# Finer first units, larger unit groups where two layers meet, and copies that go to ScalarE first

## The chip, the cores and the metric

The kernel runs on one core of one Trainium2 chip. The metric is the device time of one execution in microseconds (us); a time given for a kernel is the median of several executions. Besides, one execution was recorded by the hardware profiler, and its times are those of the views below. Engines go by short names: PE is TensorE (PEld its weight loads), DVE is VectorE, ACT is ScalarE, SP is SyncE, whose queue issues the loads.

## The reference

Two layers run one after the other on 256 tokens of 2048 numbers. Each layer normalizes x over its 2048 numbers, scales and shifts it by vectors made from a conditioning vector c (h), projects h to 6144 columns, runs two branches on them, projects the concatenation of both back to 2048 columns, normalizes that and adds it, gated, to x:

```python
    mod = (c @ w_ada + b_ada)[:, None, :]
    shift, scale, gate = jnp.split(mod, 3, axis=-1)
    h = rms_norm(x, g_pre) * (1 + scale) + shift
    z = h @ w_in
    u, g_pool, q, k, v, g_diff = jnp.split(z, splits, axis=-1)
    pool_out = multiscale_pool(u, w_pool, pool_scale) * jax.nn.silu(g_pool)
    ...
    diff_out = att.reshape(B, S, D_DIFF) * jax.nn.silu(g_diff)
    y = jnp.concatenate([pool_out, diff_out], axis=-1) @ w_out
    return x + (1 + gate) * rms_norm(y, g_post)
```

So a layer cannot start before the one ahead of it has ended for a token: its norm needs all 2048 numbers of y, and h needs the norm of the new x. Everything is float32; the result is (256, 2048).

## The kernel before, in words

**Tiles.** The 256 tokens are two row tiles of 128 (`st` 0 and 1). The 2048 rows of a weight matrix are 16 k tiles of 128; two neighbouring k tiles are one `kp`. The columns come in blocks of 512: 12 blocks (`nb`) for w_in, 4 for w_out. A *unit* is one kp of one block, 128 x 1024 numbers, 512 KB. For each unit SP loads a tile `raw`, ScalarE rounds it to a short float (`whi`, CAST), VectorE makes the rest (`wlo` = raw - whi), and TensorE multiplies: per k tile and row tile the three products hi*hi, hi*lo and lo*hi, 12 products of 128x512 per unit. The left operand `h` is split into hi and lo as well: x is scaled by its row's norm (`xnt`), transposed on TensorE into a bank of PSUM (`psb`), and ScalarE applies the k tile's scale A and shift B twice (`hz`, then `hft`), from which VectorE makes the lo part.

**Modulation.** The vectors shift, scale and gate are 48 pieces of 128 per layer, each made by two reductions on VectorE of loaded tiles of w_ada (`adaz`, 512 KB each) with the spread c (`cb`). A k tile of h needs four such tiles, then three small instructions (A, A, B).

**Visits.** The modulation comes in little by little, so kp after kp becomes available. The planner (`plan`) goes round the 12 blocks and takes as many kp as there are. Each such *visit* of a block has one sum of 128x512 per row tile in PSUM (`accc`, four of them): sums are copied out to SBUF at a visit's end (`zz`) and copied in again (`accc<-zz`) when the block's next visit starts. Such copies go to VectorE or ScalarE, whichever the planner holds less loaded (`lighter`, `copy`).

**Order.** The order of instructions on each engine is written out ahead of time, by a planner in the program (`Flow`): parts of the kernel are tasks, each with a due time, and a cost model chooses which task issues next on an engine. Each engine then executes its list in order and waits on semaphores. `need(u, before)` is the due time so many us ahead of TensorE's use of unit u. Buffers come from `Slots`: 34 large SBUF tiles for raw, whi, wlo, w_ada, h and results, with shares by kind.

**The turn.** In the last visit of w_out (four units), all products of row tile 0 come ahead of those of row tile 1 (`group`), and so they do for the first four units of layer 1. At a row tile's last product follow: a square with a sum on ScalarE (`sqj`) and the gating (`yz`) on VectorE, a norm of about ten tiny steps on VectorE (`rs`, `rx`, `ry`, `rh`), four updates of x, squares of x, another norm (`rms`), and `half_h`, which scales, transposes and modulates 256 columns of this row tile. Its due times before were those of the units that use it.

**The start.** SP loads c, x and eight w_ada tiles, then the weights. The squares of x go in eight pieces to whichever engine is lighter, one norm serves both row tiles, and `make_h` makes the first kp for both.

## Time and profile before

| what | value |
|---|---|
| median of 3 runs | 863.91 us (862.27 to 865.26) |
| profiled execution, its own time | 866.97 us |
| its span, first to last instruction | 865.2 us |
| mean granted TensorE clock | 0.977 |
| TensorE busy | 802.3 us, 93% |
| VectorE busy | 742.6 us, 86% |
| ScalarE busy | 509.9 us, 59% |
| loaded from HBM | 242.17 MB |

In the profile every instruction has one line (L125, the place in the planner that issues it), so groups go by the names of tiles: `accc<-whiz,hz` is a product of layer input and rounded weights into a sum, `accc<-whiz,catz` one of w_out, `psb<-consts,xnt` a transpose of scaled x. In rows of the timeline stand the start, the length, the engine, the operation, what is written from what, and in brackets how long the engine had been idle and what ended that. Matmuls are pipelined: the starts tell the pace, the lengths overlap. A row of the table by stretches has the busy time of each engine in it, the granted clock, the share of the DMA engines and what they moved.

### The profile page before, as it was taken

How to read it: one execution, taken by the hardware profiler on the slowest of the kernel's cores; microseconds unless marked ns; L12 is line 12 of the kernel's file. 1: busy time of each engine (PE TensorE's matmuls, PEld its weight loads, DVE VectorE, ACT ScalarE, POOL GpSimd, SP SyncE). 2: the span in 40 equal slices, each digit the busy share in tenths (PEclk: the TensorE clock that was granted, in tenths of full speed). 3: DMA queues.
4: the chain of work that ended last, by engine and by line, in shares of the span. 5: the costliest groups of instructions: out<-in, count | busy, mean ns of one | idle time of the engine just before them, and what ended most of it. 6: DMA issues, size and time to landing. Idle time of an engine off the chain costs nothing.

```text
span 865.2 us, 11872 instructions
## 1 busy us (share of the span) xinstructions
PE 802.3 (93%) x4058; PEld 667.1 (77%) x4058; DVE 742.6 (86%) x1375; ACT 509.9 (59%) x871; POOL 0.2 (0%) x4
## 2 busy tenths in 40 slices
PE   3699999999999999999719999999999999999995
PEld 1588888879788887888607788787888788788884
DVE  6999999999999989999998898998657697787335
ACT  4777787567455687654467544546544684784341
POOL 0000000000000000000000000000000000000000
PEclk9999999999999999999958999999999999999998
DMA  9988899999999667689966999999666444636602
GB/s 344 410 341 300 315 370 390 393 339 404 403 327 402 246 206 276 195 323 393 348 227 225 361 364 381 382 398 358 226 203 212 147 126 149 230 115 193 210 0 98
DMA packets 68239, 245.08 MB, mean 283 GB/s; under 512 B 7729, under 2 KB 8017, under 8 KB 67665
## 3 DMA queue, kind: packets, MB, share of 16 engines
q1 hardware_dynamic: 67890, 244.14, 78.3%
q8 instruction: 32, 0.52, 0.2%
q14 instruction: 29, 0.24, 0.1%
q10 hardware_dynamic: 288, 0.17, 0.1%
HBM read 242.17 MB, written 2.11 MB: 282 GB/s over the span
## 4 chain that ended last, share of the span: by engine, by line
PE 37%; DVE 8%; DMA 4%; issue 2%; ACT 2%; DVEq 0%; SPq 0%; ACTq 0%
PE accc L125 33%; PE psb L125 4%; DVE adaz L125 3%; DVE wloz L125 3%; DMA rawz<-in_w_in 2%; DMA adaz<-in_w_ada 2%; DVE x L125 1%; DVE yz L125 0%; ACT xnt L125 0%; ACT whiz L125 0%; ACT hz L125 0%; DVE rh L125 0%; ACT hft L125 0%; DVE ry L125 0%; ACT zz L125 0%
## 5 line engine op out<-in xcount | busy, mean ns | idle before, releaser
L125 PE MATMUL accc<-whiz,hz 128*128 128x512 f32 x1280 | 408.2, 396 | 2.1 <-ACT hz L125 2.0
L125 ACT CAST whiz<-rawz 128x1024 fp32r<-128x1024 f32 x256 | 264.3, 1051 | 97.8 <-DMA rawz<-in_w_in 49.8
L125 DVE TENSOR_TENSOR wloz<-rawz,whiz 128x1024 fp32r<-128x1024 f32 x256 | 305.9, 1218 | 15.6 <-ACT whiz L125 12.7
L125 PEld LDWEIGHTS accc<-whiz,hz 128*128 128x128 f32 x1280 | 242.0, 190 | 54.4 <-ACT hz L125 2.9
L125 PE MATMUL accc<-wloz,hz 128*128 128x512 f32 x640 | 253.1, 396 | 1.6 <-DVE wloz L125 1.6
L125 DVE SCALAR_TENSOR_TENSOR adaz<-adaz,cb 128x1024 f32<-128x1024 f32 x192 | 229.2, 1218 | 7.2 <-DMA adaz<-in_w_ada 5.3
L125 PE MATMUL accc<-whiz,catz 128*128 128x512 f32 x512 | 161.1, 393 | 0.0
L125 PEld LDWEIGHTS accc<-wloz,hz 128*128 128x128 f32 x640 | 121.6, 190 | 27.7 <-DVE wloz L125 3.5
L125 PEld LDWEIGHTS accc<-whiz,catz 128*128 128x128 f32 x512 | 95.4, 188 | 19.2 <-issue 0.3
L125 PE MATMUL accc<-wloz,catz 128*128 128x512 f32 x256 | 100.5, 393 | 0.0
L125 ACT COPY zz<-accc 128x512 f32<-128x512 f32 x100 | 57.6, 587 | 65.8 <-PE accc L125 63.7
L125 ACT COPY accc<-zz 128x512 f32<-128x512 f32 x82 | 48.3, 595 | 42.7 <-DVE rtt L125 26.9
L125 PE MATMUL accc<-hz,whiz 128*128 128x256 f32 x512 | 72.1, 283 | 0.0
L125 PEld LDWEIGHTS accc<-hz,whiz 128*128 128x128 f32 x512 | 66.9, 191 | 1.1
L125 PEld LDWEIGHTS accc<-wloz,catz 128*128 128x128 f32 x256 | 48.2, 188 | 10.2 <-issue 0.5
L125 PE MATMUL psb<-consts,xnt 128*128 128x128 f32 x64 | 13.4, 326 | 44.7 <-ACT xnt L125 34.6
L125 PEld LDWEIGHTS psb<-consts,xnt 128*128 128x128 f32 x64 | 8.8, 163 | 50.1 <-ACT xnt L125 39.0
L125 DVE COPY accc<-zz 128x512 f32<-128x512 f32 x44 | 30.1, 687 | 17.7 <-ACT zz L125 17.5
L125 PE MATMUL accc<-hz,wloz 128*128 128x256 f32 x256 | 42.0, 284 | 0.0
L125 DVE COPY zz<-accc 128x512 f32<-128x512 f32 x42 | 28.6, 685 | 8.3 <-PE accc L125 8.2
L125 PEld LDWEIGHTS accc<-hz,wloz 128*128 128x128 f32 x256 | 35.5, 192 | 0.0
L125 DVE TENSOR_TENSOR yz<-accc,Gwg 128x512 f32<-128x512 f32 x16 | 10.7, 687 | 27.9 <-ACT sqj L125 27.8
(104 smaller groups left out, 556.2 us busy)
## 6 DMA issues: line engine op xcount, KB each, us to landing
adaz<-in_w_ada SPq DMA_DIRECT2D x192, 512.0 KB, 7.1
rawz<-in_w_in SPq DMA_DIRECT2D x192, 512.0 KB, 6.7
rawz<-in_w_out SPq DMA_DIRECT2D x64, 512.0 KB, 4.4
x<-in_x SPq DMA_DIRECT2D x2, 1024.0 KB, 8.1
Gwg<-in_w_pool SPq DMA_DIRECT2D x8, 256.0 KB, 8.1
Gwg<-gate SPq DMA_DIRECT2D x2, 1024.0 KB, 5.3
out<-x SPq DMA_DIRECT2D x8, 256.0 KB, 2.8
band<-in_band SPq DMA_DIRECT2D x1, 544.0 KB, 6.9
```

Source lines behind the costliest of these rows:

```text
L125: return f(*args, **kw)
```

## The change

The planner gets other rules and numbers; what is computed stays.

- The first three units (`TURN[0]`, all of kp 0) form a group that goes by single k tiles: k tile 0 with row tile 0, then row tile 1, then k tile 1. Their weights are loaded in halves (`first_loads`), and x's second row tile is loaded behind the first four w_ada tiles. Each row tile has its own squares, norm and `half_h`. Casts and wlo of these units go by halves (`pieces`).
- Where the layers meet, the last two visits of w_out (eight units) form a group, and the first nine units of layer 1 (three kp of three blocks; `START[1]`, `TURN[1]`), sorted by kp. The third pair of sums of such a group takes banks of the transposes.
- `end_out`, `residual` and `half_h` at the turn have fixed early due times (-3, -2, -2.5) and so go ahead of everything else that an engine could issue.
- A copy goes to VectorE only if the planner has it more than 0.5 us behind ScalarE's time.
- The order of w_in's blocks (`ORDERS`) is another, w_out starts with the attention's kp (`HALVES`), the slot shares and some constants of the cost model differ.

```diff
@@ -357,10 +360,11 @@
         self.a, self.out = a, out
         pool = lambda name, **kw: ctx.enter_context(tc.tile_pool(name=name, bufs=1, **kw))
         self.cp, self.sp = pool("cp"), pool("sp")
-        self.big = Slots(f, pool("zp"), "z", self.BIG, raw=3, w=6, ada=3)
+        self.big = Slots(f, pool("zp"), "z", self.BIG, raw=3, hi=3, lo=3, ada=2)
         self.tmp = Slots(f, pool("tp"), "t", self.TMP)
         self.wide = Slots(f, pool("gp"), "g", 1)
         self.banks = Slots(f, pool("psp", space=PSUM), "b", self.BANKS)
+
         self.accs = Slots(f, pool("accp", space=PSUM), "c", self.ACCS)
         self.dp = pool("dp", space=bass.MemoryType.DRAM)
         self.names = 0
...
@@ -380,11 +384,13 @@
         return self.banks.take([P, 512], "ps")
 
 
-    START = [1, 2]
+    START = [1, 3]
+
+    TURN = [3, 9]
     RATE = {(0, 2): 0.82, (1, 2): 0.85, (0, 0): 0.92, (0, 1): 0.9, (1, 0): 0.8, (1, 1): 0.35}
-    ORDERS = [[6, 4, 8, 10, 2, 0, 7, 5, 9, 11, 3, 1]] * 2
-
-    HALVES = ((0, 4), (4, 8))
+    ORDERS = [[6, 4, 7, 5, 2, 8, 9, 3, 10, 11, 0, 1]] * 2
+
+    HALVES = ((4, 8), (0, 4))
 
     def plan(self):
 
...
@@ -443,17 +449,18 @@
                 for kp in range(k0, k1):
                     u = Unit("w_out", l, nb, 2 * kp, kp == k0 and (not late or nb < 2), kp == k1 - 1 and (late or nb < 2), nb < 2 and late)
                     u.end = late
-                    if n == 7:
-                        u.group = 2 * l + 1
+                    if n >= 6:
+                        u.group = 2 * l + 2
                     units.append(u)
                     if n < 6:
                         earn(self.RATE[l, 1])
             while l + 1 < DEPTH and kp_at[l + 1][self.START[l + 1] - 1] is None:
                 take()
-        for l in range(1, DEPTH):
+        for l, n in enumerate(self.TURN):
             i = next(i for i, u in enumerate(units) if u.l == l)
-            for u in units[i : i + 4]:
-                u.group = 2 * l
+            units[i : i + n] = sorted(units[i : i + n], key=lambda u: u.k)
+            for u in units[i : i + n]:
+                u.group = 2 * l + 1
         return units
 
     def lay_out(self):
...
@@ -466,20 +473,24 @@
             while g and i + n < len(self.units) and self.units[i + n].group == g:
                 n += 1
             us = self.units[i : i + n]
-            for sts in ([[0], [1]] if g else [[0, 1]]):
-                self.steps += [(u, sts) for u in us]
+            if g == 1:
+
+                self.steps += [(u, [st], [0]) for st in range(NST) for u in us] + [(u, [0, 1], [1]) for u in us]
+            else:
+                for sts in ([[0], [1]] if g else [[0, 1]]):
+                    self.steps += [(u, sts, [0, 1]) for u in us]
             i += n
         for i, u in enumerate(self.units):
             if u.first:
                 open_[u.w, u.nb] = Visit(u, i)
                 self.visits.append(open_[u.w, u.nb])
             u.visit = open_[u.w, u.nb]
-            u.left = NST
+            u.left = 2 * NST
         for n in range(len(self.steps) - 1, -1, -1):
             self.steps[n][0].step = n
         self.cum = [0.0]
-        for u, sts in self.steps:
-            self.cum.append(self.cum[-1] + 1.36 * len(sts))
+        for u, sts, ks in self.steps:
+            self.cum.append(self.cum[-1] + 0.68 * len(sts) * len(ks))
         self.first_use, self.uses = {}, {}
         for u in self.units:
             key = u.w, u.l, u.k // 2
...
@@ -530,20 +540,20 @@
-        for st in range(NST):
-            nc.sync.dma_start(self.x[st], a["x"][st * P : (st + 1) * P, :])
+        self.arrived = [False] * NST
+        f.spawn(self.first_loads, -95.0)
-            f.spawn(lambda st=st: self.first_squares(st), -80.0 + st)
+            f.spawn(lambda st=st: self.first_squares(st), -85.0)
-        f.spawn(self.rope_tables, -60.0)
-        f.spawn(self.mask, -50.0)
+        f.spawn(self.rope_tables, self.need(self.first_end[0]["w_in"], 60.0))
+        f.spawn(self.mask, self.need(self.first_end[0]["w_in"], 60.0))
...
@@ -556,6 +566,31 @@
             f.spawn(lambda l=l: self.load_pool_weights(l))
             for kp in range(8):
                 f.spawn(lambda l=l, kp=kp: self.make_h(l, kp), self.need_h(l, kp, 4.0))
+
+    def first_loads(self):
+
+        us = [u for u in self.units if u.group == 1]
+
+        def x(st):
+            self.nc.sync.dma_start(self.x[st], self.a["x"][st * P : (st + 1) * P, :])
+            self.arrived[st] = True
+
+        def raw(u, i):
+            self.nc.sync.dma_start(tiles[u][:, i], self.a[u.w][u.l, u.nb][:, u.k + i])
+            u.raw = tiles[u]
+
+        tiles = {u: self.big.take([P, 2, NB], "raw", kind="raw") for u in us}
+        x(0)
+        for e in self.adas[:4]:
+            self.ada_tile(e)
+        raw(us[0], 0)
+        x(1)
+        for u in us[1:]:
+            raw(u, 0)
+        for e in self.adas[4:8]:
+            self.ada_tile(e)
+        for u in us:
+            raw(u, 1)
 
     def spread_c(self):
 
...
@@ -669,7 +704,7 @@
     def lighter(self):
 
         now = self.f.now
-        return "vector" if now["vector"] < now["scalar"] else "scalar"
+        return "vector" if now["vector"] + 0.5 < now["scalar"] else "scalar"
 
     def copy(self, out, x):
         if self.lighter() == "vector":
...
@@ -722,6 +757,8 @@
+        if e in self.adas[:8]:
+            return [-81.0, -6.0, -6.0, -6.0, -4.0, -4.0, -4.0, -4.0][self.adas.index(e)]
...
@@ -785,14 +826,22 @@
-        for j in range(4):
-            self.square(0, st, j)
-        self.squared[0][st] = 1
-        if all(self.squared[0]):
-            s1 = self.small([P, NST], "xs1")
-            self.nc.vector.tensor_reduce(s1, self.xss[0], axis=AX.X, op=ALU.add)
-            r = self.rsqrt(s1, NST, 1.0 / D)
-            self.xr[0] = [r[:, st : st + 1] for st in range(NST)]
+        f, x, ss = self.f, self.x[st], self.xss[0]
+        f.wait(lambda: self.arrived[st])
+        n = D if st == 0 else D // 2
+        junk = self.big.take([P, D], "junk", BF16)
+        self.nc.scalar.activation(junk[:, 0:n], x[:, 0:n], AF.Square, accum_out=ss[:, st, 0:1])
+        self.big.give(junk)
+        if st:
+
+            junk = self.big.take([P, n], "junk")
+            self.nc.vector.scalar_tensor_tensor(junk, x[:, n:], 1.0, x[:, n:], op0=ALU.mult, op1=ALU.mult, accum_out=ss[:, st, 1:2])
+            self.big.give(junk)
+            f.due(-4.5)
+            self.xr[0][st] = self.rms(ss[:, st, 0:2])
+        else:
+            f.due(-80.0)
+            self.xr[0][st] = self.rsqrt(ss[:, st, 0:1], 1, 1.0 / D)
...
@@ -806,14 +855,14 @@
-        early = l and kp < self.START[l]
-
-        f.wait(lambda: self.gated[l - 1][0] >= 2 and self.made[l] > 2 * kp + bool(early) if l else not kp or self.made[l] > 2 * kp)
+        early = kp < self.START[l]
+
+        f.wait(lambda: self.gated[l - 1][0] >= 2 and self.made[l] > 2 * kp + bool(early) if l else early or self.made[l] > 2 * kp)
-                f.spawn(lambda st=st: self.half_h(l, kp, st, hi, lo), self.need_h(l, kp, 6.0))
+                f.spawn(lambda st=st: self.half_h(l, kp, st, hi, lo), st + 0.1 * kp - (2.5 if l else 5.5))
...
@@ -848,21 +897,35 @@
         self.tmp.give(xn)
         hf = self.tmp.take([P, 2, P], "hf")
         c = slice(st * P, (st + 1) * P)
+
+        def rest(i):
+            nc.vector.tensor_tensor(lo[:, i, c], hf[:, i, :], hi[:, i, c].bitcast(F32), op=ALU.subtract)
+            self.h_lo.add((l, 2 * kp + i, st))
+
         for i in range(2):
             kt = 2 * kp + i
+            f.wait(lambda: self.made[l] > kt)
             self.modulated(hi[:, i, c], l, kt, b[:, i * P : (i + 1) * P])
             self.h_hi.add((l, kt, st))
             self.modulated(hf[:, i, :], l, kt, b[:, i * P : (i + 1) * P])
+            if not l:
+                rest(i)
         self.banks.give(b)
-        for i in range(2):
-            nc.vector.tensor_tensor(lo[:, i, c], hf[:, i, :], hi[:, i, c].bitcast(F32), op=ALU.subtract)
-            self.h_lo.add((l, 2 * kp + i, st))
+        if l:
+            rest(0), rest(1)
         self.tmp.give(hf)
 
 
+    def pieces(self):
+
+        us = [u for u in self.units if u.group == 1]
+        return [(u, slice(i, i + 1)) for i in range(2) for u in us] + [(u, slice(0, 2)) for u in self.units if u.group != 1]
+
     def load(self):
 
         for u in self.units:
+            if u.group == 1:
+                continue
             self.f.due(self.need(u, 7.0))
             raw = self.big.take([P, 2, NB], "raw", kind="raw", keep=4)
             self.nc.sync.dma_start(raw, self.a[u.w][u.l, u.nb][:, u.k : u.k + 2, :])
...
@@ -870,22 +933,26 @@
 
     def cast(self):
 
-        for u in self.units:
-            self.f.due(self.need(u, 1.5))
+        for u, ks in self.pieces():
+            self.f.due(-5.0 + 1.5 * ks.start if u.group == 1 else self.need(u, 1.5))
             self.f.wait(lambda: u.raw is not None)
-            hi = self.big.take([P, 2, NB], "whi", F32R, kind="w", keep=4)
-            self.nc.scalar.copy(hi, u.raw)
-            u.hi = hi
+            self.f.wait(lambda: self.big.count.get("hi", 0) - self.big.count.get("lo", 0) < 4)
+            if u.hi is None:
+                u.hi = self.big.take([P, 2, NB], "whi", F32R, kind="hi", keep=3)
+            self.nc.scalar.copy(u.hi[:, ks], u.raw[:, ks])
+            u.hi_of |= set(range(2)[ks])
 
     def rest(self):
 
-        for u in self.units:
-            self.f.due(self.need(u, -0.2))
-            self.f.wait(lambda: u.hi is not None)
-            lo = self.big.take([P, 2, NB], "wlo", F32R, kind="w", keep=4)
-            self.nc.vector.tensor_tensor(lo, u.raw, u.hi.bitcast(F32), op=ALU.subtract)
-            self.big.give(u.raw)
-            u.lo = lo
+        for u, ks in self.pieces():
+            self.f.due(-5.0 + 1.5 * ks.start if u.group == 1 else self.need(u, -0.2))
+            self.f.wait(lambda: ks.start in u.hi_of)
+            if u.lo is None:
+                u.lo = self.big.take([P, 2, NB], "wlo", F32R, kind="lo", keep=1)
+            self.nc.vector.tensor_tensor(u.lo[:, ks], u.raw[:, ks], u.hi[:, ks].bitcast(F32), op=ALU.subtract)
+            u.lo_of |= set(range(2)[ks])
+            if ks.stop == 2:
+                self.big.give(u.raw)
 
     def prepare(self):
 
...
@@ -893,7 +960,8 @@
-                acc = self.accs.take([P, NB], "acc")
+                wide = u.group % 2 and not v.more and [w for w in self.visits if w.l == v.l and self.units[w.at].group == u.group].index(v) > 1
+                acc = (self.banks if wide else self.accs).take([P, NB], "acc")
...
@@ -902,13 +970,13 @@
-        for n, (u, sts) in enumerate(self.steps):
+        for n, (u, sts, ks) in enumerate(self.steps):
-            self.mm(u, sts)
-            u.left -= len(sts)
+            self.mm(u, sts, ks)
+            u.left -= len(sts) * len(ks)
...
@@ -917,25 +985,25 @@
-            if u.last and sts:
+            if u.last and ks[-1] and sts:
-                f.spawn(lambda u=u, sts=sts: end(u, sts), self.need(self.units[nxt.at], 3.0))
+                f.spawn(lambda u=u, sts=sts: end(u, sts), -3.0 if u.group and u.w == "w_out" else self.need(self.units[nxt.at], 3.0))
-    def mm(self, u, sts):
+    def mm(self, u, sts, ks):
-        for i in range(2):
+        for i in ks:
-            f.wait(lambda: have(self.h_hi, kt) and u.hi is not None)
+            f.wait(lambda: have(self.h_hi, kt) and i in u.hi_of)
-            if turned or u is self.units[0]:
+            if turned or u.group == 1:
...
@@ -1017,7 +1088,7 @@
-            self.accs.give(acc[st])
+            self.give_sum(acc[st])
```

33 lines of the change are left out of this document (20 added, 13 removed).

## The prediction

> **What bounds the kernel now.** I read the page first: busy shares, then the row of granted clock.
>
> ```profile
> span 865.2 us, 11872 instructions
> PE 802.3 (93%) x4058; PEld 667.1 (77%) x4058; DVE 742.6 (86%) x1375; ACT 509.9 (59%) x871; POOL 0.2 (0%) x4
> ...
> PEclk9999999999999999999958999999999999999998
> ```
>
> TensorE is busy 93% of the span, and its clock is full except in one place just past the middle. So the time is TensorE's work plus the holes in it. The list of waits says whom the holes belong to (total us, times, longest), and one row of it, ScalarE's, is for later:
>
> ```profile
> PE psb L125 <- ACT xnt L125: 34.6, 6, 12.0
> PE psb L125 <- DVE xnt L125: 10.0, 1, 10.0
> ...
> ACT whiz L125 <- DMA rawz<-in_w_in: 49.8, 39, 4.8
> ```
>
> Nearly all are waits of transposes (psb) for a normalized piece of x (xnt). The table by stretches shows where (busy us of PE, weight loads, DVE, ACT, POOL; clock; DMA share; GB/s):
>
> ```profile
> 0.00:20.00 20.00, 7.63 (x9) 2.67 (x9) 13.50 (x60) 8.70 (x17) 0.20 (x4) 1.00 0.90 340
> 20.00:40.00 20.00, 10.93 (x48) 8.81 (x49) 18.30 (x31) 12.86 (x17) 0.00 (x0) 1.00 1.03 409
> ...
> 100.00:120.00 20.00, 20.00 (x103) 17.06 (x102) 19.85 (x34) 16.23 (x26) 0.00 (x0) 1.00 1.02 371
> ...
> 420.00:440.00 20.00, 8.38 (x37) 6.28 (x35) 19.37 (x52) 9.96 (x20) 0.00 (x0) 0.75 0.95 350
> 440.00:460.00 20.00, 6.93 (x21) 5.09 (x22) 17.63 (x46) 13.81 (x34) 0.00 (x0) 0.50 0.46 157
> ```
>
> Holes: the start, and the turn from layer 0 to layer 1. Between them TensorE is full, but so is VectorE (19.85 of 20 us), and the DMA engines are full at the start and at 100 us: gains must not ask more of these two. One product of 128x512 is issued every 0.227 us at full clock, from a piece of the chain that ended last (start, length, count):
>
> ```profile
> 784.02 71.24 PE accc L125 x314
> ```
>
> A unit, 12 such products, is thus 2.72 us, and half of it (one row tile) 1.36 us.
>
> **The start.** The timeline of the first 41 us:
>
> ```profile
> 8.65 0.69 DVE L125 SCALAR_TENSOR_TENSOR junkt<-x 128x512 f32<-128x512 f32 x1 [2.78 <-DMA x<-in_x]
> ...
> 9.95 0.58 ACT L125 COPY cb<-psb 128x512 f32<-128x512 f32 x1 [1.12 <-PE psb L125]
> ...
> 23.24 1.05 ACT L125 CAST whiz<-rawz 128x1024 fp32r<-128x1024 f32 x1 [4.81 <-DMA rawz<-in_w_in]
> ...
> 24.52 1.04 ACT L125 CAST whiz<-rawz 128x1024 fp32r<-128x1024 f32 x1 [0.23 <-DMA rawz<-in_w_in]
> ...
> 25.00 1.22 DVE L125 SCALAR_TENSOR_TENSOR adaz<-adaz,cb 128x1024 f32<-128x1024 f32 x1
> ...
> 26.72 0.34 DVE L125 TENSOR_SCALAR xnt<-x,ry 128x256 f32<-128x256 f32 x1
> ...
> 29.36 0.56 ACT L125 ACTIVATE hz<-psb,B,A 128x256 fp32r<-128x256 f32 x1
> 29.97 2.13 PE L125 MATMUL accc<-whiz,hz 128*128 128x512 f32 x4 [1.95 <-ACT hz L125]
> ...
> 40.41 0.40 PE L125 MATMUL accc<-whiz,hz 128*128 128x512 f32 x1
> ```
>
> The first product comes at 29.97, three units are done at 40.4. One scaling of x (26.72) waits on VectorE behind eight reductions of modulation tiles (adaz), although four suffice for the first k tile. VectorE there, before:
>
> ```order
> L125 SCALAR_TENSOR_TENSOR adaz_136,mod_96<-adaz_136,cb_84 128x1024
> L125 SCALAR_TENSOR_TENSOR adaz_138,mod_96<-adaz_138,cb_84 128x1024
> L125 SCALAR_TENSOR_TENSOR A_98<-mod_96,b_108 128x1
> L125 TENSOR_TENSOR A_98<-A_98,cols_90 128x1
> L125 SCALAR_TENSOR_TENSOR B_100<-mod_96,cols_90 128x1
> L125 TENSOR_SCALAR xnt_232<-x_10_93,ry_220 128x256
> ```
>
> and in the change, around the first three values A, A, B (ry_207 is row tile 0's norm; the last of eight tiny steps stands first here):
>
> ```order
> L126 SCALAR_TENSOR_TENSOR ry_207<-rh_206,ry_207 128x1
> L126 SCALAR_TENSOR_TENSOR adaz_130,mod_94<-adaz_130,cb_84 128x1024
> L126 SCALAR_TENSOR_TENSOR adaz_132,mod_94<-adaz_132,cb_84 128x1024
> L126 SCALAR_TENSOR_TENSOR adaz_134,mod_94<-adaz_134,cb_84 128x1024
> L126 SCALAR_TENSOR_TENSOR A_96<-mod_94,b_107 128x1
> L126 TENSOR_TENSOR A_96<-A_96,cols_90 128x1
> L126 SCALAR_TENSOR_TENSOR B_98<-mod_94,cols_90 128x1
> L126 TENSOR_TENSOR wloz_248<-rawz_103,whiz_138 128x512
> ```
>
> The first product now needs one row tile's norm, four tiles and half a weight tile. Sum: ScalarE's copies of c end at 10.5 (9.95 + 0.58); the square of 2048 columns, estimated from the 1024-column cast, 2.1, to 12.6; eight small steps of about 0.22 to 14.5; three reductions at 1.15 from start to start to 17.9; A, A, B 0.6; then hz 0.4: first product at 19, 11 us earlier. The loads allow it: 512 KB land every 1.28 us (23.24 to 24.52), and behind x (8.65) four such tiles and a quarter megabyte of weights land by about 14.7. But x's second half now queues behind them on SP's ring and lands near 17.4; its square, norm and scaling then share VectorE with the small wlo pieces and give row tile 1 its first product near 25.5. The second k tile needs the next four reductions, which stand behind that norm: 24.1 to 29.0, A and B to 29.6, products from 30.1 on, all 36 of the three units done near 35.0. So 11 us at the first product are worth **5.4 us** at the third unit (40.4 - 35.0). Bounds: 8 if VectorE has less in its way; 1.5 if the extra small instructions and the late second half cost what three reductions do.
>
> **The turn.** The timeline, all engines:
>
> ```profile
> 426.88 0.39 PE L125 MATMUL accc<-whiz,catz 128*128 128x512 f32 x1
> ...
> 432.81 2.74 DVE L125 SCALAR_TENSOR_TENSOR x<-yz,ry,x 128x512 f32<-128x512 f32 x4
> ...
> 438.29 0.91 ACT L125 ACTIVATE xnt<-x,ry 128x256 f32<-128x256 f32 x2 [1.48 <-DVE ry L125]
> 438.86 1.11 PE L125 MATMUL psb<-consts,xnt 128*128 128x128 f32 x4 [11.59 <-ACT xnt L125]
> ...
> 446.89 1.21 DVE L125 SCALAR_TENSOR_TENSOR adaz<-adaz,cb 128x1024 f32<-128x1024 f32 x1
> ...
> 451.41 1.31 ACT L125 ACTIVATE xnt<-x,ry 128x256 f32<-128x256 f32 x3 [5.56 <-DVE ry L125]
> 451.97 1.11 PE L125 MATMUL psb<-consts,xnt 128*128 128x128 f32 x4 [12.00 <-ACT xnt L125]
> 453.21 0.80 PE L125 MATMUL accc<-whiz,hz 128*128 128x512 f32 x1
> ...
> 461.63 0.62 PE L125 MATMUL accc<-whiz,hz 128*128 128x512 f32 x2
> ```
>
> Two waits of 11.59 and 12.00 us, then half clock. From 427.1 to 462.1 are 35.0 us, in which 16 products (3.6 us) and 16 transposes (1.11 for four at half clock, so about 2 at full) get done: **29.4 us lost**. The second wait is one of order. TensorE before, at the end of layer 0 (catz) and the start of layer 1 (hz):
>
> ```order
> L125 MATMUL accc_4044<-whiz_3999,catz_3722 128x512
> L125 MATMUL psb_4285<-consts_86,xnt_4281 128x128 x2
> L125 MATMUL psb_4287<-consts_86,xnt_4282 128x128 x2
> L125 MATMUL psb_4353<-consts_86,xnt_4345 128x128 x2
> L125 MATMUL psb_4355<-consts_86,xnt_4346 128x128 x2
> L125 MATMUL accc_4124<-whiz_4095,hz_4036 128x512
> ```
>
> The other row tile's transposes (4353, 4355) stand ahead of all products of the first. In the change its first ones (psb_4382) come after 26 products of layer 1:
>
> ```order
> L126 MATMUL psb_4252<-consts_86,xnt_4243 128x128 x2
> L126 MATMUL accc_4106<-whiz_4027,hz_4057 128x512
> ```
>
> ```order
> L126 MATMUL accb_4274<-whiz_4235,hz_4058 128x512
> L126 MATMUL psb_4382<-consts_86,xnt_4376 128x128 x2
> L126 MATMUL psb_4384<-consts_86,xnt_4377 128x128 x2
> L126 MATMUL accb_4274<-wloz_4326,hz_4058 128x512
> ```
>
> The chain itself, where nothing else is on VectorE, is read at the end of the kernel:
>
> ```profile
> 854.86 0.39 PE L125 MATMUL accc<-whiz,catz 128*128 128x512 f32 x1
> ...
> 858.57 2.74 DVE L125 SCALAR_TENSOR_TENSOR x<-yz,ry,x 128x512 f32<-128x512 f32 x4
> ```
>
> Last product to first update of x: 3.7 us. Update to scaled x: 432.81 to 438.29, 5.5. Scaled x to product: 451.41 to 453.21, 1.8. Together 11.0. Eight units of one row tile now follow row tile 0's last product, 8 x 1.36 = 10.9 us: its chain is just covered, less what is put into it (two weight casts on ScalarE, one wlo): I take 1.5 us of wait. Row tile 1's chain is 9.8 us up to its transposes (3.7, 5.5 and 438.29 to 438.86); one wlo and six small lo parts stand in it, which I take as two rows like that at 446.89, 2.6: about 12.4. It has 1.5 us of that wait and 26 products, 5.9, plus transposes and lo waits of about 1.5: that leaves **3.5 us**, by this count. The clock comes on top, since short holes cost it too:
>
> ```profile
> 178.78 0.95 PE L125 MATMUL psb<-consts,xnt 128*128 128x128 f32 x4 [1.43 <-ACT xnt L125]
> ...
> 493.68 0.95 PE L125 MATMUL psb<-consts,xnt 128*128 128x128 f32 x4 [1.85 <-ACT xnt L125]
> ...
> 495.00:496.00 1.00, 1.00 (x4) 0.81 (x3) 1.00 (x2) 0.86 (x2) 0.00 (x0) 0.50 1.02 414
> ```
>
> After 1.43 us the clock stayed; after 1.85 it was halved in the second that follows, for some 3.4 us, so 1.6 lost. I add 1.6 once. Turn after: 1.5 + 3.5 + 1.6 = 6.6, **23 us saved**; bounds 16 (another 7 us of wait) and 27 (2.6 left). The Trainium skill ("TensorE: Matmul & The Clock Gate", the clock gate) puts the drop after about 3.4 us of idleness in a free-running window; the row at 493 shows it after 1.85. By the page the 1.6 would not fall due and the time would be 1.6 lower.
>
> **The copies.** Groups, busy us and mean ns:
>
> ```profile
> L125 ACT COPY zz<-accc 128x512 f32<-128x512 f32 x100 | 57.6, 587 | 65.8 <-PE accc L125 63.7 <-DVE adaz L125 1.5
> L125 ACT COPY accc<-zz 128x512 f32<-128x512 f32 x82 | 48.3, 595 | 42.7 <-DVE rtt L125 26.9 <-DVE zz L125 14.0 <-PE accc L125 0.8
> ...
> L125 ACT ACT_TABLE_LOAD x10 | 12.8, 1283 | 5.2 <-DMA cb<-in_c 2.7 <-DVE sm L125 2.3
> ...
> L125 DVE COPY accc<-zz 128x512 f32<-128x512 f32 x44 | 30.1, 687 | 17.7 <-ACT zz L125 17.5
> L125 DVE COPY zz<-accc 128x512 f32<-128x512 f32 x42 | 28.6, 685 | 8.3 <-PE accc L125 8.2
> ```
>
> In the change's order VectorE keeps 17 and 15 of the last two, so 54 x 0.69 = 37 us leave it; ScalarE gets 22 more, 13 us, the rest are gone because three kp share one visit. ScalarE also gets four more table loads, 5.1 us. At 59% busy it holds both, so I cost them at nothing; without that cover they are 18 us. The skill ("ScalarE: Activation LUTs", on ACT_TABLE_LOAD) gives 2.66 us per switch with its drain; the rows here show 1.28. By the page ScalarE would carry 10.6 us there, still under cover. VectorE's relief buys little directly, since TensorE waits only about 5 us outside start and turn; but it keeps the earlier start from running into a full VectorE. Order of blocks and halves, slot shares, three more load issues, the two sums that take transposes' banks, and the tail stand at nothing: nothing in the trace waits for a bank, and the tail's chain has the same instructions. Plus or minus 4 for all of it, about what TensorE now waits outside start and turn.
>
> **Sum**: 5.4 + 23 = 28.4 off 865.2, span 836.8. The profiled run took 866.97 with its surroundings, 3.1 above the median shown (863.91), so against that median: **835.5 us**.
>
> **Rivals.** (1) *The turn's wait only moves.* Row tile 1's transposes still stand at a fixed place, and casts ahead of the scaling wait for loads. Seven to ten us more wait: 844. For it: VectorE and DMA stay full up to 440; against: the chain has priority now. (2) *The link takes the start back.* DMA share is 1.02 at 100 us, with 371 GB/s; weights asked 5 us earlier may not come earlier: 841. Against: the bytes asked for by 35 us are nearly the same, and it moved 409 GB/s when it had to. (3) *Better*: VectorE's 37 us end the 5 us of small waits and shorten both chains; 5 + 2 + 3.5 more: 825. (4) *Slower: ScalarE's queue.* Copies in and out of the sums now stand behind casts that wait for weights: 39 waits, 49.8 us, 1.28 each. With four sums only, such a wait reaches TensorE. Eating 28.4 and 2.6 more needs 24 of them, nearly half of the 55 reloads that the change has (110 copies for two row tiles): then 867. Against: in 100 to 120 us ScalarE is busy 16.2 of 20 us and TensorE never waits. (5) *It does not do what it says*: half-tile casts and transposes are ordered as planned but both stalls stay: 863; the order above speaks against it.
>
> **Numbers.** Forecast 0.51, (1) 0.15, (2) 0.12, (3) 0.14, (4) 0.06, (5) 0.02. Range: best ends 8 + 27 + 4 = 39 off the median's 864 give 825, worst 1.5 + 16 - 4 = 13.5 give 850; with a little beyond either end 822 to 852. The forecast and rivals 1 to 3 are all faster by over 0.3% (2.6 us, about what tells from no change here): 0.92; same 0.02; slower 0.06.
>
> **What would show it.** First product at 18 to 21 us, three units done by 34 to 37. No wait of a transpose at the turn over 5 us, their sum under 8, two separate ones, the second for xnt of row tile 1. The clock row shows at most one slice below 9 in the middle. VectorE busy near 705 us, ScalarE near 528. TensorE waits elsewhere still near 5 us. It is wrong if a wait of TensorE for wloz, whiz or zz appears between 100 and 300 us, or if the turn keeps over 14 us.

## The result, and the profile after

The changed kernel takes **869.72 us** (867.77 to 870.90) against 863.91 (862.27 to 865.26) before: ratio 1.0065, 95% interval 1.0045 to 1.0085. It is slower by 0.65%, where 835.5 us were predicted. Medians leave out runs in the chip's slower state, which only E2 below had: one of its four, the profiled one, so its waits are of that run. The page of the changed kernel:

```profile
span 866.0 us, 11893 instructions
PE 810.9 (94%) x4058; PEld 669.4 (77%) x4058; DVE 714.7 (83%) x1314; ACT 529.9 (61%) x917; POOL 0.2 (0%) x4
PEclk9999999999999999999999989999979999999998
```

VectorE and ScalarE are near where they were forecast (705 and 528 us), and the hole past the middle is gone from the clock row. In its place there are two dents, further right. The start, in the timeline of TensorE after (start, length, what it waited for in brackets):

```profile
18.89 0.80 PE L126 MATMUL accc<-whiz,hz 128*128 128x512 f32 x1 [3.33 <-ACT hz L126]
...
34.02 0.62 PE L126 MATMUL accb<-wloz,hz 128*128 128x512 f32 x2
34.47 0.39 PE L126 MATMUL accc<-whiz,hz 128*128 128x512 f32 x1
```

The first product comes at 18.89, and at 34.47 the three units are done and the next one begins (forecast 19 and 35.0). The turn, same view:

```profile
436.07 0.44 PE L126 MATMUL psb<-consts,xnt 128*128 128x128 f32 x2 [1.66 <-ACT xnt L126]
437.93 0.50 PE L126 MATMUL accc<-whiz,hz 128*128 128x512 f32 x1 [0.97 <-ACT hz L126]
...
448.34 0.84 PE L126 MATMUL psb<-consts,xnt 128*128 128x128 f32 x4 [2.32 <-ACT xnt L126]
450.53 0.61 PE L126 MATMUL psb<-consts,xnt 128*128 128x128 f32 x2 [0.62 <-ACT hft L126]
```

Two separate waits, for row tile 0 and row tile 1, and their followers: 5.6 us in these four rows, where before had 24.6 us of waits for xnt between 430 and 460. Both gains are there. The table by stretches shows where they went (busy us of PE, weight loads, DVE, ACT, POOL, each with its count; clock; DMA share; GB/s). Before:

```profile
40.00:240.00 200.00, 197.78 (x1015) 168.72 (x1015) 195.63 (x322) 139.50 (x206) 0.00 (x0) 1.00 0.96 362
240.00:420.00 180.00, 179.63 (x934) 147.85 (x933) 171.64 (x348) 113.26 (x224) 0.00 (x0) 1.00 0.84 298
420.00:480.00 60.00, 35.31 (x165) 28.67 (x164) 54.78 (x129) 36.58 (x74) 0.00 (x0) 0.74 0.74 263
480.00:660.00 180.00, 175.80 (x889) 148.42 (x888) 149.68 (x217) 89.78 (x119) 0.00 (x0) 0.99 0.89 324
```

After:

```profile
40.00:240.00 200.00, 191.34 (x971) 161.35 (x970) 179.06 (x286) 147.91 (x230) 0.00 (x0) 0.99 0.96 356
240.00:420.00 180.00, 177.70 (x930) 145.89 (x929) 165.29 (x331) 117.52 (x228) 0.00 (x0) 1.00 0.79 287
420.00:480.00 60.00, 53.93 (x232) 42.68 (x231) 54.25 (x115) 43.85 (x85) 0.00 (x0) 0.97 0.73 257
480.00:660.00 180.00, 166.10 (x819) 140.43 (x819) 152.00 (x230) 84.14 (x113) 0.00 (x0) 0.95 0.95 343
```

At 420 to 480 TensorE's idle time falls from 24.7 us to 6.1, and the clock rises from 0.74 to 0.97. But from 40 to 240 it sits idle 8.7 us instead of 2.2, and from 480 to 660 13.9 instead of 4.2, at a clock of 0.95. In instructions: 67 more issued at the turn, 44 and 70 fewer in the two stretches. VectorE, which was full from 40 to 240 (195.6 of 200 us), now has holes there (179.1), although it has the modulation still to do. Its waits say for what. The list of waits after (total us, times, longest):

```profile
ACT whiz L126 <- DVE wloz L126: 52.5, 29, 3.9
DVE adaz L126 <- DMA adaz<-in_w_ada: 45.7, 44, 3.2
...
ACT whiz L126 <- DVE adaz L126: 28.5, 20, 3.8
...
PE psb L126 <- ACT xnt L126: 19.6, 9, 5.5
...
PE psb L126 <- DVE rtt L126: 7.5, 3, 4.5
```

The same rows before:

```profile
ACT whiz L125 <- DVE adaz L125: 11.7, 9, 3.6
ACT whiz L125 <- DVE wloz L125: 9.4, 10, 2.1
...
DVE adaz L125 <- DMA adaz<-in_w_ada: 5.3, 8, 1.5
```

VectorE's waits for loads of modulation tiles (adaz) went from 5.3 us to 45.7, the waits of ScalarE's casts for these two kinds of work on VectorE from 21.1 to 81.0. One such chain, in the timeline after, all engines:

```profile
503.16 1.23 DVE L126 SCALAR_TENSOR_TENSOR adaz<-adaz,cb 128x1024 f32<-128x1024 f32 x1 [2.65 <-DMA adaz<-in_w_ada]
506.71 1.04 ACT L126 CAST whiz<-rawz 128x1024 fp32r<-128x1024 f32 x1 [3.81 <-DVE adaz L126]
508.99 1.04 ACT L126 CAST whiz<-rawz 128x1024 fp32r<-128x1024 f32 x1 [1.24 <-DVE adaz L126]
509.94 0.91 ACT L126 ACTIVATE xnt<-x,ry 128x256 f32<-128x256 f32 x2
510.50 1.30 PE L126 MATMUL psb<-consts,xnt 128*128 128x128 f32 x4 [5.52 <-ACT xnt L126]
```

VectorE stands 2.65 us for a tile that has not landed. Casts on ScalarE stand until VectorE has finished reductions of adaz tiles; a cast reads nothing of these, so what it waits for is a buffer that they release. The scaling of x (xnt) stands behind the casts in ScalarE's list, and TensorE waits 5.52 us for it. The row names xnt; the cause is three engines away.

### The profile page after: what moved, and what is told of

Its sections match the earlier page's. It is cut to its first block, busy times and chain, and to the rows that moved or that the text cites. A ratio compares the mean times of both kernels' runs of the same rounds, so it can differ in the third digit from the quotient of the medians.

```text
span 866.0 us, 11893 instructions
## 1 busy us (share of the span) xinstructions
PE 810.9 (94%) x4058; PEld 669.4 (77%) x4058; DVE 714.7 (83%) x1314; ACT 529.9 (61%) x917; POOL 0.2 (0%) x4
## 5 line engine op out<-in xcount | busy, mean ns | idle before, releaser
L126 PE MATMUL accc<-whiz,hz 128*128 128x512 f32 x1248 | 404.0, 399 | 8.4 <-ACT hz L126 6.3
L126 ACT CAST whiz<-rawz 128x1024 fp32r<-128x1024 f32 (+1 forms) x259 | 265.1, 1045 | 142.6 <-DVE wloz L126 52.5
L126 DVE TENSOR_TENSOR wloz<-rawz,whiz 128x1024 fp32r<-128x1024 f32 (+1 forms) x259 | 308.1, 1209 | 31.4 <-ACT whiz L126 22.2
L126 PEld LDWEIGHTS accc<-whiz,hz 128*128 128x128 f32 x1248 | 236.8, 191 | 61.7 <-ACT hz L126 7.9
L126 DVE SCALAR_TENSOR_TENSOR adaz<-adaz,cb 128x1024 f32<-128x1024 f32 x192 | 232.9, 1221 | 48.3 <-DMA adaz<-in_w_ada 45.7
L126 PE MATMUL accc<-wloz,hz 128*128 128x512 f32 x624 | 248.0, 398 | 0.0
L126 PE MATMUL accc<-hz,whiz 128*128 128x256 f32 x512 | 75.8, 287 | 0.0
L126 ACT COPY accc<-zz 128x512 f32<-128x512 f32 x93 | 53.7, 603 | 27.9 <-DVE rtt L126 20.7
L126 ACT ACTIVATE hz<-psb,B,A 128x256 fp32r<-128x256 f32 (+1 forms) x40 | 21.2, 530 | 38.2 <-DVE B L126 32.3
L126 ACT ACTIVATE pt<-psb,sm 128x128 f32<-128x128 f32 (+1 forms) x64 | 26.5, 421 | 12.1 <-DVE sm L126 8.1
L126 DVE TENSOR_TENSOR yz<-accc,Gwg 128x512 f32<-128x512 f32 x16 | 10.9, 688 | 23.7 <-ACT sqj L126 23.6
```

What stands on the lines that cost most here:

```text
L126: return f(*args, **kw)
```

## The experiments

**Theories.** *1, the buffers:* the edit of the slot shares guarantees two buffers instead of three to tiles of w_ada; the modulation's loads are then too late. *2, the copy rule* sends copies to ScalarE and so makes xnt late there. *3, the block order* holds buffers longer. *4, scatter:* the planner's order is a draw, and another draw would take another time. Each run was timed beside the kernel before on the same chip; that kernel's medians there were 864.7 to 866.0 us. The runs came in batches on different chips, so a difference of 2 us between batches is no difference, and there the ratios are the safer guide.

### One part undone at a time

The changed kernel, with the old copy rule:

```diff
-        return "vector" if now["vector"] + 0.5 < now["scalar"] else "scalar"
+        return "vector" if now["vector"] < now["scalar"] else "scalar"
```

> The changed kernel with the copy rule of before (VectorE or ScalarE, whichever is free first). Theory 1 (the buffers: two instead of three for tiles of w_ada, so VectorE waits in order for loads) expects no cure: 862 to 875 us, TensorE still waits for xnt and rtt between 120 and 420 and between 490 and 650 us for 15 us or more in sum, VectorE for loads of adaz over 30 us. Theory 2 (the copies sent to ScalarE first make xnt late there) expects 845 to 855 us and the waits for xnt from ScalarE (19.6 us) at 5 or less. Theory 3 (the block order holds buffers longer) expects 865 to 873.

With the old block order and halves:

```diff
-    ORDERS = [[6, 4, 7, 5, 2, 8, 9, 3, 10, 11, 0, 1]] * 2
-    HALVES = ((4, 8), (0, 4))
+    ORDERS = [[6, 4, 8, 10, 2, 0, 7, 5, 9, 11, 3, 1]] * 2
+    HALVES = ((0, 4), (4, 8))
```

> The changed kernel with the block order and halves of before. Theory 1 expects the waits for loads of adaz on VectorE to stay over 30 us and the time over 860. Theory 3 (block order) expects 845 to 855 us, with the losses at 120 to 200 and 490 to 650 us gone. Theory 2 expects 865 to 873.

That, and the third buffer:

```diff
-raw=3, hi=3, lo=3, ada=2)
+raw=3, hi=3, lo=3, ada=3)
```

> As the run beside it (block order and halves of before), and three buffers for tiles of w_ada instead of two. Theory 1 expects VectorE's waits for loads of adaz back under 15 us and a time at least 8 us below the run with two. Theories 2 and 3 expect the same time as with two, within 3 us.

The kernel before, with one buffer fewer:

```diff
-raw=3, w=6, ada=3)
+raw=3, w=6, ada=2)
```

> The kernel before with one number changed: two buffers for tiles of w_ada instead of three. Theory 1 expects 872 to 885 us, with VectorE's waits for loads of adaz up from 5 to 30 us or more and new waits of TensorE outside start and turn of 8 us or more. Theories 2 and 3 expect 862 to 867, as before.

| run | us | ratio to before (95%) | VectorE waits for adaz, us | last adaz load issued, us |
|---|---|---|---|---|
| before (3 buffers) | 863.91 | 1 | 5.3 | 586.0 |
| changed (2) | 869.72 | 1.0065 (1.0045 to 1.0085) | 45.7 | 646.9 |
| E1 changed, old copy rule (2) | 891.25 | 1.0312 (1.0258 to 1.0366) | 31.0 | 681.0 |
| E2 changed, old order (2) | 881.46 | 1.0196 (1.0143 to 1.0249) | 48.0 | 660.3 |
| E3 changed, old order (3) | 854.15 | 0.9873 (0.9815 to 0.9932) | 15.9 | 599.7 |
| E4 before (2) | 888.12 | 1.0286 (1.0263 to 1.0309) | 32.5 | 602.9 |

One number in the kernel before costs 24 us (E4, 3 us over its range), and the same number gives 27.3 back in the changed one with the old order (E2 to E3; the expectations below have 29.7 and 14, with all four runs of E2). The runs of E1, E2 and E3 spread over 10 to 12 us each, so these differences are rough. Theories 2 and 3 fall with the wrong sign: undoing either edit makes the kernel slower, by 21.5 and 11.7 us. E1 was meant to show no effect by theory 1 and missed its range by 16 us, so the copy rule matters in a way that this theory does not hold. The row of waits in E4, against 5.3 before:

```profile
DVE adaz L125 <- DMA adaz<-in_w_ada: 32.5, 36, 2.3
```

### The buffer alone, in the changed kernel

With a third buffer among 34 and its own block order the changed kernel's planner finds no order at all, because every task ends up waiting. So E5 and E6 have 35 large buffers (and 10 temporaries for 12) with three and with two for w_ada; E7 keeps 34 and moves shares from the weights; E8 moves a cost in the planner's model by 0.2%.

E5, of which E6 has the first pair of lines alone:

```diff
-    BIG, TMP, BANKS, ACCS = 34, 12, 4, 4
+    BIG, TMP, BANKS, ACCS = 35, 10, 4, 4
...
-raw=3, hi=3, lo=3, ada=2)
+raw=3, hi=3, lo=3, ada=3)
```

E7:

```diff
-raw=3, hi=3, lo=3, ada=2)
+raw=3, hi=2, lo=2, ada=4)
```

E8:

```diff
-"scalar": (0.085, 0.89e-3, 0.13, 0.15)
+"scalar": (0.085, 0.888e-3, 0.13, 0.15)
```

> The changed kernel with its own block order and copy rule, three buffers for tiles of w_ada, 35 large buffers instead of 34 (with 34 the order finds no way through) and 10 temporaries instead of 12 to make room. Theory 1 (too few buffers for w_ada make VectorE wait in order for loads) expects 833 to 848 us: the 29.7 us that the third buffer was worth under the old block order (883.9 to 854.2), less the 14 us that the new order is worth already with two. VectorE's waits for loads of adaz fall from 45.7 to under 20 us, TensorE's waits outside start and turn to under 10. If the loss of the change had another cause, it stays at 862 to 872.

> The same 35 large buffers and 10 temporaries with two buffers for tiles of w_ada: the control. Theory 1 expects 862 to 875 us with VectorE's waits for loads of adaz over 30 us. If only the number of large buffers matters (theory 1b: any 35th buffer would do), 835 to 850 us.

> The changed kernel with 34 large buffers, shares 2 for the rounded weights, 2 for the rests and 4 for tiles of w_ada. Theory 1 expects VectorE's waits for loads of adaz under 15 us and 840 to 860 us. If the weights' shares are what is short (theory 1c), more waits of ScalarE's casts and 870 or more.

> The changed kernel with one cost of the planner moved by 0.2% (0.888 instead of 0.89 ns an element on ScalarE): nothing but the order moves. If the order's scatter is small, 866 to 874 us. If the planner's order scatters (theory 4: the loss of 0.65% is a draw), more than 1% off the changed kernel, either way.

| run | us | ratio to before (95%) | VectorE waits for adaz, us | last adaz load issued, us |
|---|---|---|---|---|
| E5 (35, three) | 851.83 | 0.9859 (0.9825 to 0.9892) | 9.2 | 590.4 |
| E6 (35, two) | 882.51 | 1.0209 (1.0185 to 1.0233) | 48.5 | 656.1 |
| E7 (34, shares 2, 2, 4) | 846.08 | 0.9801 (0.9757 to 0.9845) | 2.2 | 567.5 |
| E8 (order moved) | 870.08 | 1.0081 (1.0051 to 1.0111) | 42.7 | 645.8 |

E5 against E6 is the clean pair: one buffer, 30.7 us. E5 missed its own range (833 to 848) by 4. E6 shows that more buffers in all do not help; it missed its range (862 to 875) by 7.5 and is 12.8 us slower than the changed kernel, so with two buffers other details weigh much, perhaps the two temporaries fewer. E7 has no buffer more than the changed kernel and is 23.6 us faster. E8 issues in another order (its page has 1316 instructions on VectorE and 915 on ScalarE, for 1314 and 917) and takes the same time, so theory 4 falls too, as far as one draw tells. The three rows of E5, E6 and E7:

```profile
DVE adaz L126 <- DMA adaz<-in_w_ada: 9.2, 13, 2.1
```

```profile
DVE adaz L126 <- DMA adaz<-in_w_ada: 48.5, 38, 4.2
```

```profile
DVE adaz L126 <- DMA adaz<-in_w_ada: 2.2, 4, 0.9
```

### Start, turn and the queue, with enough buffers

E9 takes the larger groups and the early due times out of E7, E10 the new start. E11 is the changed kernel with the w_ada loads on another queue. E12 is the kernel before with four buffers guaranteed to w_ada, as in E7, and two fewer to the weights.

E9, from E7 (the due times of `end_out` and `half_h` go back in the same way, and so does the sorting by kp):

```diff
-    START = [1, 3]
+    START = [1, 2]
-    TURN = [3, 9]
+    TURN = [3, 4]
-                    if n >= 6:
+                    if n == 7:
...
-f.spawn(lambda st=st: self.residual(l, st), -2.0)
+f.spawn(lambda st=st: self.residual(l, st), self.need(self.steps[min(self.at + 4, len(self.steps) - 1)][0]))
```

E10, from E7 (the squares, the rope tables and the mask also as before):

```diff
-        f.spawn(self.first_loads, -95.0)
+        for st in range(NST):
+            nc.sync.dma_start(self.x[st], a["x"][st * P : (st + 1) * P, :])
...
-        for l, n in enumerate(self.TURN):
+        for l, n in list(enumerate(self.TURN))[1:]:
```

E11, from the changed kernel:

```diff
-        self.nc.sync.dma_start(w, self.a["w_ada"][l, nt][:, i * D // 2 : (i + 1) * D // 2])
+        self.nc.gpsimd.dma_start(w, self.a["w_ada"][l, nt][:, i * D // 2 : (i + 1) * D // 2])
```

E12, from before:

```diff
-raw=3, w=6, ada=3)
+raw=3, w=4, ada=4)
```

> The run with shares 2, 2 and 4 (846.1 us), with the turn of before: two row-split units there instead of three groups, four units of layer 1 instead of nine ahead of the other row tile, the norms' chains at their old due times. If the turn is worth what it was predicted to be once buffers suffice: 866 to 872 us (846 and 20 to 26), with two waits of 9 us or more for xnt near 430. If the rest of the kernel fills what the turn loses (the link catches up while TensorE waits), 850 to 860.

> The same run with the start of before: both row tiles of x, all norms and eight modulation tiles ahead of the first unit, whole weight tiles. If the start is worth what was predicted: 850 to 853 us (846 and 4 to 7). If the link takes the start back (rival 2 of the prediction): 845 to 848.

> The changed kernel, two buffers for tiles of w_ada, whose loads are issued from GpSimd's queue, so that a load that waits for its buffer holds back no weight load on SyncE's queue. Theory 1 in the form 'two buffers carry too few tiles' (7 us of landing and 1.2 of reduction a tile on two buffers is 4.1 us a tile where the plan needs 3.05) expects no cure: 862 to 880 us, last load of a tile after 640 us. In the form 'the waiting load blocks SyncE's queue for the weights' it expects 845 to 858.

> The kernel before with the same lean to w_ada: four weight buffers and four for tiles of w_ada instead of six and three. If before was already held by its buffers, 850 to 860 us; if three sufficed there, 862 to 868, and then what the run at 846.1 gained over before is the change's own.

| run | us | ratio to before (95%) |
|---|---|---|
| E9 (E7 without the larger groups) | 846.68 | 0.9769 (0.9743 to 0.9795) |
| E10 (E7 without the new start) | 843.65 | 0.9737 (0.9711 to 0.9762) |
| E11 (changed, w_ada by GpSimd) | 913.28 | 1.0535 (1.0481 to 1.0590) |
| E12 (before, shares 4 and 4) | 861.62 | 0.9945 (0.9924 to 0.9966) |

**The start is worth nothing here.** E10 has its first product at 24.48 us against 18.47 in E7, and is no slower; by the medians it is 2.4 us faster, and so a little under both its ranges. The table by stretches of E7 and then of E10 shows where the lead is given back:

```profile
60.00:140.00 80.00, 77.03 (x378) 64.01 (x378) 76.36 (x130) 71.33 (x119) 0.00 (x0) 1.00 0.99 370
```

```profile
60.00:140.00 80.00, 79.25 (x403) 67.22 (x402) 78.25 (x136) 75.21 (x128) 0.00 (x0) 1.00 1.00 391
```

The DMA engines are busy throughout in both (0.99 and 1.00), and E10 moves 391 GB/s to 370. In 80 us it issues 25 more instructions on TensorE, some 5.7 us at 0.227: about what its first product is late. Why E7 moves less there is open.

**The larger groups.** E9's time says that together with the early due times they are worth nothing, against the 20 to 26 expected, and lies under both expectations. But E9's waits do not show the old turn either: TensorE waits 10.8 us between 418 and 470, against 24.8 in E12 and 6.9 in E7. Something else had shortened it; that was taken up next. E12 says that three buffers nearly sufficed before: a fourth is worth 2.3 us there by the medians and 0.55%, 4.8 us, beside the kernel before on its chip, so most of E7's lead over before is the change's own.

**The queue** is not settled. E11 has no cure: VectorE waits 73.5 us for adaz, and the last load is issued at 684.9. That is the sign that two buffers predict, but the time lies 33 us over the range that went with it. The run carries a cost of its own (first product at 27.21 us), so it does not rule out that a waiting load also holds back weights on SP.

### Which edit brings the rest

E12 to E7 is 15.5 us that the shares do not explain. E13 is E12 with the new halves alone:

```diff
-    HALVES = ((0, 4), (4, 8))
+    HALVES = ((4, 8), (0, 4))
```

E14 is E7 with the old copy rule (the edit of E1), E15 is E7 and E18 is E10 with the old order and halves (the edit of E2), E17 is E12 with the new copy rule alone (E1's edit backwards). E16 is E10 with the old groups, its chains as early as in the change:

```diff
-    START = [1, 3]
+    START = [1, 2]
...
-                    if n >= 6:
+                    if n == 7:
...
-        for l, n in list(enumerate(self.TURN))[1:]:
+        for l, n in [(1, 4)]:
```

> The kernel before with shares 4 and 4 (861.6 us) and one more edit, the changed kernel's halves (the upper half of k of w_out first). In its order 24 products of row tile 0 stand ahead of row tile 1's transposes at the turn, where before had three, without any larger group. If the halves carry the turn's second wait: that wait of 12 us goes to under 4, and the time is 847 to 853 us. If the larger groups carry it: 858 to 864.

> The run with shares 2, 2 and 4 (846.1 us) with the copy rule of before. With two buffers the new rule was worth 21 us. If copies to ScalarE first help only where VectorE waits in order for loads, 845 to 849 us; if the rule is a gain of its own, 855 to 868. The prediction's cost of nothing expects 844 to 848.

> The same run (846.1 us) with the block order and halves of before, the larger groups kept. The prediction's cost of nothing for both expects 842 to 850. With two buffers the new order was worth 14 us; with three, the nearest pair is 851.8 and 854.2. If the order holds buffers shorter and that is its worth, 848 to 852.

> The run without the new start (843.7 us), with the groups at the turn as before, urgent chains and halves kept: in its order six products stand between the two row tiles' transposes, where the run has 27. If what is lost at the turn is caught up later because loads are ahead by then: 842 to 846, with a wait of 6 us or more for xnt at the turn. If the turn's waits count in full: 850 to 856.

> The kernel before with shares 4 and 4 (861.6 us) and the changed kernel's copy rule alone. If the rule is a gain of its own, as undoing it (858.6 against 846.1) says: 847 to 853 us, VectorE busy 25 us less. If it gains only together with the change's order: 859 to 864. The prediction's cost of nothing expects 860 to 863; its rival 4 (copies behind casts on ScalarE) 865 or more.

> The fastest so far (843.7 us: shares 2, 2 and 4, larger groups, new copy rule, start of before) with the block order and halves of before. If these are worth nothing once buffers suffice, as 847.7 against 846.1 says: 842 to 847 us. If the new order is worth its few us only without the new start: 848 to 853.

| run | us | against | difference, us | ratio to before (95%) |
|---|---|---|---|---|
| E13 new halves alone | 868.76 | E12 861.62 | +7.1 | 1.0035 (1.0016 to 1.0054) |
| E14 old copy rule | 858.59 | E7 846.08 | +12.5 | 0.9922 (0.9903 to 0.9941) |
| E15 old order and halves | 847.66 | E7 846.08 | +1.6 | 0.9794 (0.9766 to 0.9822) |
| E16 old groups | 850.07 | E10 843.65 | +6.4 | 0.9824 (0.9802 to 0.9845) |
| E17 new copy rule alone | 865.43 | E12 861.62 | +3.8 | 1.0005 (0.9984 to 1.0026) |
| E18 old order and halves | 847.19 | E10 843.65 | +3.5 | 0.9777 (0.9746 to 0.9808) |

**Halves.** The timeline of the transposes at the turn, E12 and then E13:

```profile
434.53 1.12 PE L125 MATMUL psb<-consts,xnt 128*128 128x128 f32 x4 [11.82 <-ACT xnt L125]
447.64 1.11 PE L125 MATMUL psb<-consts,xnt 128*128 128x128 f32 x4 [11.99 <-ACT xnt L125]
```

```profile
449.04 1.11 PE L125 MATMUL psb<-consts,xnt 128*128 128x128 f32 x4 [9.23 <-ACT xnt L125]
460.05 1.59 PE L125 MATMUL psb<-consts,xnt 128*128 128x128 f32 x8 [2.21 <-ACT xnt L125]
```

With the new halves alone the planner already puts 24 products of row tile 0 ahead of row tile 1's transposes, and the second wait goes from 11.99 to 2.21 us. Both of E13's ranges were missed all the same (868.76 against 864 at most): TensorE loses it again between 300 and 380 us. The rows for 340 to 380 us, E12 and then E13:

```profile
340.00:380.00 40.00, 39.88 (x205) 32.52 (x204) 38.93 (x103) 23.73 (x52) 0.00 (x0) 1.00 0.68 230
```

```profile
340.00:380.00 40.00, 34.45 (x155) 28.57 (x156) 38.15 (x87) 22.21 (x41) 0.00 (x0) 0.91 0.45 155
```

w_out now starts with the k tiles that the attention makes; that the old block order makes these late is the likely cause, argued and not shown. As a pair the two edits are worth little (E15, E18), but that little is a difference of two things. With the old order the larger groups take in a block whose products have the other order of operands (`hz,whiz`), and going by row tiles they are made in two of 128 columns for one of 256. Two rows of E15 at the turn:

```profile
447.61 1.00 PE L126 MATMUL accc<-hz,whiz 128*128 128x128 f32 x8
448.45 0.61 PE L126 MATMUL accc<-hz,wloz 128*128 128x128 f32 x4
```

The eight start within 0.84 us, 0.105 us each, hardly less than the 0.11 to 0.12 of one with 256 columns. E15 has 4142 matmuls where E7 has 4058, so some 9 us of TensorE by this estimate, and its page has it busy 814.2 us against 804.4. Yet the time is 1.6 us longer and not 9, since TensorE is idle for less of the span (31.0 us against 39.8). E2 and E3 carry the same 84 matmuls, E18 72.

**Copy rule.** Worth 12.5 us in the changed kernel with E7's shares (E14), and less than nothing in the one before (E17, 3.8 us slower; VectorE falls from 739.6 to 713.5 us busy and the time does not). E17 lies where rival 4 put it (865 or more), but its TensorE waits for xnt (38.4 us) and hardly for sums or casts (7.8 us for all accc). E12 had hardly any idle TensorE to win outside start and turn (199.8 of 200 us busy from 40 to 240). E14 for the stretch shown of E7 above:

```profile
60.00:140.00 80.00, 73.09 (x350) 60.54 (x349) 74.62 (x123) 56.30 (x88) 0.00 (x0) 0.98 0.88 316
```

TensorE is idle 6.9 us here, against 3.0 in E7. That VectorE is the limit, since the changed kernel starts its units earlier, is argued and not shown: VectorE is no busier than in E7 (74.62 us against 76.36), and the DMA engines are less so (0.88 against 0.99). For it speaks that from 40 to 420 us 12.1 of the 14.8 us that TensorE waits in E14 are for tiles that VectorE makes.

**Groups.** E16's chain waits 8.96 us where E10's longest at the turn is 1.67: 10.5 us of waits against 6.5 from 418 to 470. The time, 850.07, lies at the lower end of 'count in full'.

**The fastest** of all kernels is E10 at 843.65 us, 2.6% under before (ratio 0.9737, 0.9711 to 0.9762): the change without its start, and with four guaranteed buffers for w_ada. It is still 8 us over the forecast.

## Why the prediction was wrong, by its own steps

- **The start, 5.4 us:** right in the place (18.89 and 34.5 us for 19 and 35.0), wrong as a gain in the time. With buffers enough it is worth nothing (E10). That is the outcome that rival 2 named; its reason, the link (what the DMA engines can move), fits the full DMA engines of E7 and E10 from 60 to 140 us, but is not shown.
- **The turn, 23 us:** right in size at its place: 24.6 us of waits became 6.1 from 430 to 460 (forecast 5 of waits and 1.6 of clock). The credit was partly wrong: undoing the larger groups costs 6.4 us (E16) or, with the early due times, 0.6 (E9), and the halves, which the prediction costed at nothing, move the other row tile's transposes by themselves (E13).
- **The copies, nothing:** mis-sized. The rule is a gain: undone it costs 12.5 us with enough buffers and 21.5 without. The prediction's sentence that VectorE's relief "keeps the earlier start from running into a full VectorE" comes nearest to it, and it had no number. The table loads rose from 10 to 14 as counted, at 1283 ns each.
- **"Order of blocks and halves, slot shares, three more load issues ... stand at nothing: nothing in the trace waits for a bank"**, with plus or minus 4 us for all of it: this step failed. Order and halves are worth 2 to 4 us with enough buffers. One guaranteed buffer for w_ada is worth 24 to 31 us (E4, E2 to E3, E6 to E5). In the changed kernel itself the shares cost 17.9 us (against E5) or 23.6 (against E7), out of the 34.2 between forecast and result; the start's 5.4 are the next part, and the other 5 to 11 us are not assigned. The reason given spoke of PSUM banks; for the large buffers nothing was worked out.
- **"TensorE waits elsewhere still near 5":** the list of waits from 45 to 420 and from 460 to 700 us adds up to 24.7, against 6.6 before. Nearly all of them (21.9) are waits for xnt and rtt, not for wloz, whiz or zz, which the prediction had named as the sign of an error; the casts of the weights waited, one engine further back, on ScalarE (81.0 us, above).
- **Rival 4** gave 867, close to the time, by copies that stand behind casts on ScalarE. Its mechanism is refuted: fewer copies on ScalarE made it slower (E1), and in the changed kernel TensorE waits only 1.5 us for a copy of ScalarE into a sum. That the numbers are close is chance.

That two buffers are too few, though not the price, could have been worked out ahead from two views of before, which the prediction did not use: the page's part on DMA issues (KB each, median us to landing), and the rows on the tile adaz (shortest, median and longest ns, first and last start):

```profile
adaz<-in_w_ada SPq DMA_DIRECT2D x192, 512.0 KB, 7.1
```

```profile
L125 SPq DMA_DIRECT2D adaz<-in_w_ada x192: 327/328/1466, 2.5 to 586.0; - x192
L125 DVE SCALAR_TENSOR_TENSOR adaz<-adaz,cb x192: 1208/1218/1227, 16.4 to 593.8; 128x1024 f32<-128x1024 f32 x192
```

A tile holds its buffer from the issue of its load to the end of its reduction, by the medians 7.1 + 1.2 = 8.3 us if the reduction follows at once. Three buffers thus carry one tile in 2.8 us, two one in 4.15. The kernel issues 192 in 583.5 us, one in 3.05. Two do not suffice, three do if no tile waits. In fact tiles do wait: taking loads and reductions in order, the time from issue to the end of the reduction is 11.5 us at the median before and 9.3 in the changed kernel, and 4.2 and 3.1 tiles are held at a time. So both kernels use buffers beyond the guaranteed ones, and only these let the changed kernel come to 3.38 us a tile:

```profile
L126 SPq DMA_DIRECT2D adaz<-in_w_ada x192: 327/328/1304, 2.0 to 646.9; - x192
```

The Trainium skill ("DMA: Bandwidth & Descriptors", on the anatomy of a DMA) fits one DMA, on GpSimd's path, with a fixed 2.0 us and the bytes at 436 GB/s. For 512 KB an estimate by that page is 3.2 us. The trace agrees with its shortest landing here, 3.1 us in the changed kernel on SP's queue, but not with the median of 6.9; that other loads in flight make the difference is likely and not shown. By an estimate from the page two buffers would carry a tile in 2.2 us and suffice; the median decides.

What stays open: the gains do not add up (start, groups and the copy rule are worth different amounts beside each other), why E6 with one buffer more is slower than the changed kernel, and what the rest of the change does (the constants of the planner's cost model, the weights' one share made two), which no run undid by itself.

## What to carry to other kernels

When a change lowers a number of buffers, divide the time that one tile holds its buffer (landing by the issue rows, plus its use) by the number, and compare it with the pace at which the kernel issues such tiles. Here it was 2.8 against 3.05 us with three buffers and 4.15 with two. The quotient is the least that is needed, since tiles that wait hold longer. In lists executed in order, a late load shows up as a wait of TensorE for something unrelated, so follow it back through ScalarE's and VectorE's waits to the DMA. And a gain at one place counts only where the next limit (here, most likely, VectorE and the link) has room for the work that comes earlier.

## What the runs showed of the hardware

The clock of TensorE survived waits of 1.66 and 1.68 us in the changed kernel (at 436.07 and 549.72), and fell to 0.50 after the one of 2.32 at 448.34 with 0.62 following; before, 1.85 us had been enough. That does not make an edge between 1.7 and 1.85 us: in E1 the clock fell after a wait of 1.70 us (before 160.56), and in E4 it stayed at 1.00 through one of 2.95 (before 289.98). In the clock records the stretches at 0.50 inside the changed kernel begin at 194.7, 450.7, 508.7 and 638.4 us and last 3.41, 3.41, 6.83 and 10.24; the distances between their starts are whole multiples of 3.413 us too. So the clock is set anew on a fixed grid of that step, and how a wait lies on the grid may well decide with its length, which is not shown here. The Trainium skill ("TensorE: Matmul & The Clock Gate", the clock gate) gives an idle window of about 3.4 us. These records agree with the length of the step, but not with a need for a whole window of idleness, since 1.70 us were enough in E1.

Loads issued on GpSimd took 527 ns of it each, against 328 on SP, and landed in 7.1 us at the median against 6.9.
